# 1/sqrt in the norms: one power on GpSimd in place of nine VectorE instructions

## The chip, the cores and the metric

The kernel runs on one core of a Trainium2 chip. The metric is the device time of one execution in microseconds. The engines appear in the profile as PE (TensorE, the matmuls; PEld are its weight loads), DVE (VectorE), ACT (ScalarE), POOL (GpSimd) and SP (SyncE, which issues the DMAs). A line number such as L257 is a line of the kernel before the change.

## The reference

Two sequences of 512 tokens with 1024 channels pass through two layers that share their weights. One layer is:

```
h = RMSNorm(x);  z = h W_in, split into four groups: S5 | Hyena | RWKV-7 | neighbourhood attention
x += W_out concat_g(RMSNorm_g(mixer_g(z_g)))
x += W2 relu(W1 RMSNorm(x))^2

def rms_norm(x, g):
    y = xf * lax.rsqrt(jnp.mean(xf * xf, axis=-1, keepdims=True) + NORM_EPS)
    return y * g
```

1/sqrt of a sum over channels is wanted per token in five kinds of places: the two norms over 1024 channels of each layer, the norm of each mixer's 256 channels, the queries and keys of the attention (per head of 64 channels), the keys of RWKV (per head; here without an epsilon, with an upper limit of 1e12 on the result), and RWKV's normalisation of its output per head.

## The kernel before

Activations lie transposed: channels on the 128 partitions, tokens along the columns, 512 columns per sequence. The matrices W_in, W_out, W1 and W2 are multiplied by `mm3` in three passes of split values (high times high, high times low, low times high), each a 128x512 matmul (L1432 to L1434). `load_w` brings a block of weights; at the first use ScalarE casts the high part (L297) and GpSimd, for every fourth block VectorE, subtracts to get the low part (L298), which is also stored for the second sequence. These splits are the larger part of GpSimd's work.

Several Python generators are stepped in turn: one emits the dense stream (W_in, W_out, the MLP of both layers and sequences), one RWKV and S5, then Hyena and attention, of each sequence and layer. The program's final order on each engine isn't this one: `tile.TileContext(nc, schedule_with_timeline_sim=True)` has a planner order the instructions of every engine ahead of the run by a simulated timeline. On the chip every engine works through its own list in that order and waits at semaphores where an operand isn't ready.

A sum over channels is a sum over partitions, so it goes through TensorE. `token_rstd` multiplies squared values by a column of ones (or by a selector of the two heads) at L271, which puts tokens on the partitions: the sums of 512 tokens are 128 partitions by 4 columns, times 2 for two heads, times 2 for two chunks. L275 scales them and adds the epsilon into a tile `rsq_x`. `rsqrt` then makes `rsq_y` from it, with two helper tiles `rsq_t` and `rsq_u`, in nine small VectorE instructions (L249 to L257): a first guess by arithmetic on the bits, a step of higher order, and a Newton step. The result, tokens on partitions, has to come back to one value per column, and there are two ways: `bcast` (L293) transposes each column of `rsq_y`, repeated 128 times, on TensorE, used by the norm over 1024 channels (`norm_rstd`, whose result ScalarE copies at L1475 into the tile `R`) and by the norms of the four mixers (`group_norm`); `head_bcast` (L283) first spreads the values by a ScalarE copy and then transposes. The queries' 1/rms is used where it lies, as a scalar per partition, at L1349.

`R` scales what comes out of the next dense blocks: L1489 to L1517 for W_in, L1575 for W1. Two buffers (`pd`) take these blocks' results, so TensorE can run two blocks ahead of `R`.

Per sequence and layer there are 12 calls of `rsqrt`: two norms over 1024 channels, four mixer norms, four for queries and keys (two chunks each), and two for RWKV; with two sequences and two layers, 48.

Of the kernel before, what the change touches and what calls it, by code (L numbers as in the profile page):

```python
# [7 lines left out]
I32 = mybir.dt.int32  # L8
AF = mybir.ActivationFunctionType
ALU = mybir.AluOpType  # L10
AX = mybir.AxisListType
MUL, ADD, SUB, MAX, MIN = ALU.mult, ALU.add, ALU.subtract, ALU.max, ALU.min
P = 128
# [180 lines left out]
class Ctx:  # L194
# [46 lines left out]

    def rsqrt(self, x, n, tag):


        V = self.nc.vector
        y = self.t([P, 32], "rsq_y" + tag, 3)[:, :n]
        t = self.t([P, 32], "rsq_t" + tag)[:, :n]
        u = self.t([P, 32], "rsq_u" + tag)[:, :n]
        V.tensor_scalar(out=y.bitcast(I32), in0=x.bitcast(I32), scalar1=-0.5, scalar2=float(0x5f378000), op0=MUL, op1=ADD)  # L249
        V.tensor_tensor(out=t, in0=y, in1=x, op=MUL)  # L250
        V.tensor_tensor(out=t, in0=t, in1=y, op=MUL)
        V.tensor_scalar(out=u, in0=t, scalar1=0.3740864098072052, scalar2=-1.249273657798767, op0=MUL, op1=ADD)
        V.tensor_tensor(out=u, in0=u, in1=t, op=MUL)
        V.scalar_tensor_tensor(out=y, in0=u, scalar=1.8751890659332275, in1=y, op0=ADD, op1=MUL)
        V.scalar_tensor_tensor(out=t, in0=y, scalar=-0.5, in1=x, op0=MUL, op1=MUL)
        V.tensor_tensor(out=t, in0=t, in1=y, op=MUL)
        V.scalar_tensor_tensor(out=y, in0=t, scalar=1.5, in1=y, op0=ADD, op1=MUL)  # L257
        return y

    def token_rstd(self, srcs, ntok, sel, add, tag, sc=1.0, mulc=None):  # L260


        nc = self.nc
        nt = ntok // P
        w = sel.shape[1]
        k = 1 if w == 1 else len(srcs)
        o = self.p([P, nt, k, w], tag)
        for tt in range(nt):
            for i, s in enumerate(srcs):
                acc = w == 1  # L270
                nc.tensor.matmul(out=o[:, tt, 0 if acc else i], lhsT=s[:, tt * P:tt * P + P], rhs=sel,  # L271
                                 start=(not acc or i == 0), stop=(not acc or i == len(srcs) - 1))
        n = nt * k * w
        x = self.t([P, 32], "rsq_x" + tag, 2)[:, :n]
        nc.vector.tensor_scalar(out=x, in0=o.rearrange("p a b c -> p (a b c)"), scalar1=sc, scalar2=add,  # L275
                                op0=MUL, op1=ADD)
        return self.rsqrt(x, n, tag)

    def head_bcast(self, rn, M, tag):
# [1358 lines left out]
def trunk(tc, A, O):  # L1638
    nc = tc.nc
    base = place(nc)  # L1640
    with tc.tile_pool(name="sb", bufs=1) as sb, \
            tc.tile_pool(name="ps", bufs=1, space=bass.MemoryType.PSUM) as ps, \
            tc.tile_pool(name="dr", bufs=1, space=bass.MemoryType.DRAM) as dr:
        K = Ctx(tc, base, sb, ps, dr, A)
# [7 lines left out]
        K.zp = [K.t([P, S + 2], f"zp{b}") for b in range(2)]  # L1652
        for z in K.zp:
            nc.gpsimd.memset(z, 0.0)
        pars = [K.load_params(0)]
        zs, ys, taken, done = {}, {}, {}, set()
        xs = {(0, b): A['xT'][:, seqs[b]] for b in range(2)}
# [213 lines left out]
```

## Time and profile before

| | |
|---|---|
| median of 3 runs | 3195.2 us (3182.29 to 3195.77) |
| the profiled execution, its own time | 3179.4 us |
| its span, first to last instruction | 3177.6 us |
| mean granted TensorE clock | 0.950 of full speed |
| busy: PE, DVE, ACT, POOL | 2951.0, 1973.0, 1051.9, 828.9 us |
| HBM | 409.95 MB read, 155.83 MB written |

A busy time is the sum of an engine's instructions in the profiled execution, and its share is that of the span. In the lists of waits a row says which instruction stood, what released it, how long in total, how often, and the longest. In a timeline a row's bracket gives how long the engine had been idle ahead of it and what ended that.

### The profile page before, as it was taken

To read this page: it belongs to the slowest core of one execution; us is meant where nothing else is said; L and a number is where in the kernel's file an instruction comes from. 1 tells how busy PE (TensorE), PEld (TensorE's weight loads), DVE (VectorE), ACT (ScalarE), POOL (GpSimd) and SP (SyncE) were. 2 spreads that over 40 slices of the span, in tenths; PEclk is the share of its full clock that TensorE was granted. 3 is DMA by queue.
4 is the path that set the end of the run, shared out by engine and by line. 5 is a ranking of instruction groups with operands and counts; after the bars stand their busy time and mean duration, and the time that the engine had idled before them with its cause. 6 is when DMAs were issued, how large, how long until landed. Compare 5 with 4: busy or idle time off the path is not lost.

```text
span 3177.6 us, 48702 instructions
## 1 busy us (share of the span) xinstructions
PE 2951.0 (93%) x17328; PEld 2308.4 (73%) x17328; DVE 1973.0 (62%) x3755; ACT 1051.9 (33%) x1922; POOL 828.9 (26%) x693
## 2 busy tenths in 40 slices
PE   7987998798899998899899999998998999999999
PEld 5666776676677877767676778776776777778887
DVE  8888775785854768757627436765647457733332
ACT  5333233332322333333323223433322323332222
POOL 5642201432332336432001001312333223300000
PEclk9898999898999999999999999999999999999999
DMA  7577574365554546766655545577556445556565
GB/s 221 164 232 201 189 210 131 117 169 165 151 163 145 173 161 207 227 191 201 186 151 157 173 150 182 196 211 221 181 170 181 152 162 181 178 178 194 192 193 195
DMA packets 482840, 571.92 MB, mean 180 GB/s; under 512 B 187910, under 2 KB 238726, under 8 KB 481576
## 3 DMA queue, kind: packets, MB, share of 16 engines
q1 hardware_dynamic: 482600, 568.81, 58.4%
q8 instruction: 139, 2.28, 0.3%
q14 instruction: 101, 0.83, 0.1%
HBM read 409.95 MB, written 155.83 MB: 178 GB/s over the span
## 4 chain that ended last, share of the span: by engine, by line
PE 64%; DVE 16%; DMA 9%; issue 4%; SPq 3%; ACT 2%; POOL 1%; DVEq 0%; ACTq 0%; POOLq 0%
PE pd L1432 16%; PE pd L1434 16%; PE pd L1433 15%; DVE m L1195 2%; PE ra L677 2%; PE ra L675 2%; DMA m<-in_w_mlp 2%; PE ra L467 1%; DMA m<-in_w_in 1%; DVE m L864 1%; DVE m L530 1%; DVE m L298 1%; DMA m<-lo 1%; PE ra L1226 1%; PE ra L660 1%
## 5 line engine op out<-in xcount | busy, mean ns | idle before, releaser
L1432 PE MATMUL pd<-m,m 128*128 128x512 f32 x2984 | 1225.9, 412 | 91.7 <-ACT m L297 32.7
L1434 PE MATMUL pd<-m,m 128*128 128x512 f32 x2984 | 1210.2, 406 | 34.7 <-DMA m<-lo 23.6
L1433 PE MATMUL pd<-m,m 128*128 128x512 f32 x2984 | 1206.0, 404 | 2.3 <-DVE m L298 2.3
L1432 PEld LDWEIGHTS pd<-m,m 128*128 128x128 f32 x2984 | 580.4, 195 | 242.0 <-issue 46.0
L1434 PEld LDWEIGHTS pd<-m,m 128*128 128x128 f32 x2984 | 578.8, 194 | 176.0 <-DMA m<-lo 27.4
L1433 PEld LDWEIGHTS pd<-m,m 128*128 128x128 f32 x2984 | 580.6, 195 | 130.0 <-issue 8.0
L298 POOL TENSOR_TENSOR m<-m,m 128x512 fp32r<-128x512 f32 x282 | 395.7, 1405 | 736.5 <-ACT m L297 676.4
L1416 ACT CAST m<-m 128x512 fp32r<-128x512 f32 x376 | 232.8, 620 | 712.3 <-DMA m<-in_w_mlp 434.2
L297 ACT CAST m<-m 128x512 fp32r<-128x512 f32 (+1 forms) x400 | 256.9, 645 | 624.7 <-PE pd L1433 232.9
L1585 DVE TENSOR_TENSOR m<-pd,m 128x512 f32<-128x512 f32 x256 | 175.2, 686 | 262.6 <-PE pd L1434 262.2
L1575 DVE SCALAR_TENSOR_TENSOR do<-pd,R 128x512 f32<-128x512 f32 x128 | 87.7, 688 | 198.9 <-PE pd L1434 188.7
L1195 DVE TENSOR_TENSOR m<-m,m 128x512 f32<-128x512 f32 (+1 forms) x224 | 142.0, 677 | 4.5 <-POOL m L1195 3.6
L298 DVE TENSOR_TENSOR m<-m,m 128x512 fp32r<-128x512 f32 (+1 forms) x118 | 104.9, 889 | 62.9 <-ACT m L297 59.6
L298 DVE TENSOR_TENSOR m<-do,m 128x512 fp32r<-128x512 f32 x128 | 100.4, 786 | 62.1 <-ACT m L297 61.5
L297 ACT CAST m<-do 128x512 fp32r<-128x512 f32 x128 | 79.2, 620 | 137.0 <-DVE do L1576 136.8
L1576 DVE TENSOR_TENSOR do<-do 128x512 f32<-128x512 f32 x128 | 112.5, 880 | 3.0
L1456 POOL TENSOR_TENSOR m<-m 128x512 f32<-128x512 f32 x40 | 58.6, 1466 | 128.1 <-ACT m L1455 126.1
L1463 DVE SCALAR_TENSOR_TENSOR m<-m,par,m 128x512 fp32r<-128x512 f32 x64 | 65.1, 1026 | 34.2 <-ACT m L1462 34.1
L677 PE MATMUL ra<-m,m 128*64 128x64 f32 x512 | 77.8, 246 | 0.0
L1195 POOL TENSOR_TENSOR m<-m,m 128x512 f32<-128x512 f32 x32 | 49.2, 1540 | 98.1 <-DVE m L1195 54.9
L467 PEld LDWEIGHTS ra<-m,m 64*128 64x128 f32 x512 | 50.8, 201 | 32.5 <-issue 24.3
L675 PE MATMUL ra<-m,rw_st 64*64 64x64 f32 x448 | 73.8, 246 | 0.0
(359 smaller groups left out, 3489.9 us busy)
## 6 DMA issues: line engine op xcount, KB each, us to landing
m<-in_w_mlp SPq DMA_DIRECT2D x512, 256.0 KB, 2.9
lo<-m SPq DMA_DIRECT2D x376, 256.0 KB, 2.3
m<-lo SPq DMA_DIRECT2D x376, 256.0 KB, 2.7
m<-in_w_in SPq DMA_DIRECT2D x176, 256.0 KB, 3.5
m<-zr SPq DMA_DIRECT2D x36, 512.0 KB, 4.7
m<-in_w_out SPq DMA_DIRECT2D x64, 256.0 KB, 3.0
m<-in_xT SPq DMA_DIRECT2D x32, 256.0 KB, 4.5
zr<-do SPq DMA_DIRECT2D x32, 256.0 KB, 2.2
```

The source lines that it names most:

```text
L297: self.nc.scalar.copy(out=hi, in_=x)
L298: eng.tensor_tensor(out=lo, in0=x, in1=hi.bitcast(F32), op=SUB)
L675: nc.tensor.matmul(out=py[b0:b0 + 64, d, c], lhsT=st[b0:b0 + 64, d, c], rhs=ar[c][b0:b0 + 64, ch, 1], start=True, stop=False)
L677: nc.tensor.matmul(out=py[b0:b0 + 64, d, c], lhsT=uv[:, ch, c, q], rhs=sr[:, ch, 2 * c + q], start=st is None, stop=True)
L1195: eng.tensor_tensor(out=o, in0=a, in1=b, op=op)
L1416: nc.scalar.copy(out=hi, in_=raw)
L1432: K.nc.tensor.matmul(out=ps, lhsT=wh, rhs=hh, start=(i == 0), stop=False)
L1433: K.nc.tensor.matmul(out=ps, lhsT=wh, rhs=hl, start=False, stop=False)
L1434: K.nc.tensor.matmul(out=ps, lhsT=wl, rhs=hh, start=False, stop=(i == n - 1))
L1575: nc.vector.scalar_tensor_tensor(out=r, in0=ps, scalar=0.0, in1=R, op0=MAX, op1=MUL)
L1576: nc.vector.tensor_tensor(out=r, in0=r, in1=r, op=MUL)
L1585: nc.vector.tensor_tensor(out=x[m], in0=ps, in1=x[m], op=ADD)
```

## The change

`rsqrt` issues one GpSimd instruction, x to the power of a tile that holds -0.5, in place of the nine on VectorE. That tile is filled once at the start. Where `token_rstd` is called without an epsilon (the keys of RWKV), L275 takes the maximum with 1e-30 in place of adding 0. The helper tiles `rsq_t` and `rsq_u` are gone.

```
     def rsqrt(self, x, n, tag):
-        V = self.nc.vector
         y = self.t([P, 32], "rsq_y" + tag, 3)[:, :n]
-        t = self.t([P, 32], "rsq_t" + tag)[:, :n]
-        u = self.t([P, 32], "rsq_u" + tag)[:, :n]
-        V.tensor_scalar(out=y.bitcast(I32), in0=x.bitcast(I32), scalar1=-0.5, scalar2=float(0x5f378000), op0=MUL, op1=ADD)
-        V.tensor_tensor(out=t, in0=y, in1=x, op=MUL)
-        V.tensor_tensor(out=t, in0=t, in1=y, op=MUL)
-        V.tensor_scalar(out=u, in0=t, scalar1=0.3740864098072052, scalar2=-1.249273657798767, op0=MUL, op1=ADD)
-        V.tensor_tensor(out=u, in0=u, in1=t, op=MUL)
-        V.scalar_tensor_tensor(out=y, in0=u, scalar=1.8751890659332275, in1=y, op0=ADD, op1=MUL)
-        V.scalar_tensor_tensor(out=t, in0=y, scalar=-0.5, in1=x, op0=MUL, op1=MUL)
-        V.tensor_tensor(out=t, in0=t, in1=y, op=MUL)
-        V.scalar_tensor_tensor(out=y, in0=t, scalar=1.5, in1=y, op0=ADD, op1=MUL)
+        self.nc.gpsimd.tensor_tensor(out=y, in0=x, in1=self.mhalf[:, :n], op=ALU.pow)
         return y
 
     def token_rstd(self, srcs, ntok, sel, add, tag, sc=1.0, mulc=None):
...
-        nc.vector.tensor_scalar(out=x, in0=o.rearrange("p a b c -> p (a b c)"), scalar1=sc, scalar2=add,
-                                op0=MUL, op1=ADD)
+        nc.vector.tensor_scalar(out=x, in0=o.rearrange("p a b c -> p (a b c)"), scalar1=sc, scalar2=add or 1e-30,
+                                op0=MUL, op1=ADD if add else MAX)
         return self.rsqrt(x, n, tag)
...
             nc.gpsimd.memset(z, 0.0)
+        K.mhalf = K.t([P, 32], "mhalf")
+        nc.gpsimd.memset(K.mhalf, -0.5)
```

## Rows read from the trace of the kernel before

**Rows 1.** The page: busy us of each engine, share of the span, instructions
```profile
PE 2951.0 (93%) x17328; PEld 2308.4 (73%) x17328; DVE 1973.0 (62%) x3755; ACT 1051.9 (33%) x1922; POOL 828.9 (26%) x693
```
**Rows 2.** The page: the chain that ended last, share of the span by engine
```profile
PE 64%; DVE 16%; DMA 9%; issue 4%; SPq 3%; ACT 2%; POOL 1%; DVEq 0%; ACTq 0%; POOLq 0%
```
**Rows 3.** Stretches: length; busy us (instructions) by engine; PE clock, DMA share, GB/s
```profile
1200.00:1400.00 200.00, 175.19 (x870) 136.03 (x869) 150.39 (x260) 72.67 (x114) 103.58 (x91) 0.91 0.68 217
...
2800.00:3000.00 200.00, 196.86 (x868) 162.75 (x867) 66.16 (x103) 60.39 (x99) 2.58 (x2) 0.99 0.58 187
```
**Rows 4.** TensorE's waits: who waited <- for whom: total us, times, longest
```profile
PE pd L1432 <- DVE do L1575: 19.4, 6, 5.2
...
PE nm L293 <- DVE rsq_ynm L257: 10.5, 3, 6.2
PE pd L1434 <- POOL m L298: 10.0, 9, 3.9
...
PE ra L293 <- DVE rsq_yra L257: 2.1, 1, 2.1
...
PE nm L884 <- DVE m L864: 1.4, 1, 1.4
```
**Rows 5.** Line 257 by tile: count, duration ns min/median/max, first and last start
```profile
L257 DVE SCALAR_TENSOR_TENSOR rsq_yma<-rsq_tma,rsq_yma x24: 158/166/178, 414.1 to 2753.5; 128x8 f32<-128x8 f32 x16, 128x4 f32<-128x4 f32 x8
L257 DVE SCALAR_TENSOR_TENSOR rsq_yra<-rsq_tra,rsq_yra x15: 161/174/1271, 96.9 to 2767.9; 128x16 f32<-128x16 f32 x8, 128x4 f32<-128x4 f32 x7
L257 DVE SCALAR_TENSOR_TENSOR rsq_ynm<-rsq_tnm,rsq_ynm x9: 146/161/168, 47.7 to 2827.8; 128x4 f32<-128x4 f32 x9
```
**Rows 6.** VectorE's groups, lines 249 to 257, costliest and cheapest: busy us, mean ns
```profile
L249 DVE TENSOR_SCALAR rsq_yma<-rsq_xma 128x8 int32<-128x8 int32 (+1 forms) x24 | 7.4, 314 | 0.4
...
L250 DVE TENSOR_TENSOR rsq_tnm<-rsq_ynm,rsq_xnm 128x4 f32<-128x4 f32 x9 | 1.4, 159 | 0.2
```
**Rows 7.** Timeline at 649 us: start us, us, instruction [idle before <-releaser]
```profile
649.46 1.26 POOL L298 TENSOR_TENSOR m<-m,m 128x512 fp32r<-128x512 f32 x1 [2.94 <-ACT m L297]
649.52 1.23 DVE L253 TENSOR_TENSOR rsq_unm<-rsq_unm,rsq_tnm 128x4 f32<-128x4 f32 x1
```
**Rows 8.** Timeline at 2826 us, the last norm over 1024 channels
```profile
2825.99 0.16 DVE L275 TENSOR_SCALAR rsq_xnm<-nm 128x4 f32<-128x4 f32 x1 [4.27 <-PE nm L271]
...
2827.77 0.16 DVE L257 SCALAR_TENSOR_TENSOR rsq_ynm<-rsq_tnm,rsq_ynm 128x4 f32<-128x4 f32 x1
...
2830.26 0.60 PE L293 MATMUL nm<-c_eye,rsq_ynm 128*128 128x128 f32 x4
```
**Rows 9.** Timeline at 1223 us, the same norm in a crowded stretch
```profile
1222.89 0.15 DVE L275 TENSOR_SCALAR rsq_xnm<-nm 128x4 f32<-128x4 f32 x1
...
1223.41 2.24 POOL L298 TENSOR_TENSOR m<-m,m 128x512 fp32r<-128x512 f32 x1
...
1229.94 0.15 DVE L257 SCALAR_TENSOR_TENSOR rsq_ynm<-rsq_tnm,rsq_ynm 128x4 f32<-128x4 f32 x1
...
1230.24 1.08 PE L293 MATMUL nm<-c_eye,rsq_ynm 128*128 128x128 f32 x4 [6.16 <-DVE rsq_ynm L257]
```
**Rows 10.** GpSimd's groups by shape, one of VectorE: busy us, mean ns, idle before
```profile
L298 POOL TENSOR_TENSOR m<-m,m 128x512 fp32r<-128x512 f32 x282 | 395.7, 1405 | 736.5 <-ACT m L297 676.4 <-DMA m<-in_w_out 14.0 <-DMA m<-in_w_mlp 13.8
L667 POOL TENSOR_TENSOR rw_se<-rw_st,rw_ec 128x256 f32<-128x256 f32 x24 | 17.8, 744 | 173.2 <-DVE rw_st L668 130.9 <-DVE rw_st L664 41.9 <-DVE rw_ec L433 0.3
L1037 POOL TENSOR_TENSOR m<-m,m 128x1024 f32<-128x1024 f32 x4 | 10.5, 2622 | 28.9 <-DVE m L1036 15.3 <-DVE na_m L1352 13.6
L427 POOL MEMSET m<- 128x16 f32 x16 | 2.3, 146 | 69.8 <-PE ra L660 22.2 <-PE ra L286 18.0 <-DVE m L450 8.4
...
L298 DVE TENSOR_TENSOR m<-m,m 128x512 fp32r<-128x512 f32 x94 | 73.0, 776 | 45.0 <-ACT m L297 41.7 <-DMA m<-in_w_in 1.4 <-DMA zr<-do 1.2
```
**Rows 11.** GpSimd's waits: who waited <- for whom: total us, times, longest
```profile
POOL m L298 <- ACT m L297: 676.4, 193, 22.9
```

## The prediction

> **What bounds the kernel now.** I read the busy times first: TensorE works 93% of the span, VectorE 62%, GpSimd 26% [rows 1]. The span is 3177.6 us, so TensorE stands idle for 3177.6 - 2951.0 = 226.6 us in all; no change that leaves the matmuls alone can give back more than that. The chain of waits comes next: 64% of it is TensorE, 16% VectorE, 1% GpSimd [rows 2]. VectorE is therefore not the bound, but a part of TensorE's idle time is spent waiting for it. 16% of 3177.6 is about 510 us, against 1973 us of busy VectorE: one microsecond of VectorE in four lies on that chain. Third, the table by stretches shows where the rest can be found: between 1200 and 1400 us VectorE is busy 150 of 200 us and TensorE idles 25; between 2800 and 3000 us VectorE is busy 66 and TensorE idles 3 [rows 3]. The relief can only come from stretches of the first kind. Last, TensorE's own waits [rows 4]: the rows that name a VectorE instruction other than the ones removed are 16, the largest 19.4 us (the hidden layer's evacuation), the smallest 1.4 us, together 95 us. Those that name the removed instructions are the transposes that spread 1/rms over the columns: 10.5 us in three places (longest 6.2) and 2.1 us in one, 12.6 us in four.
>
> **What goes.** Each of the 48 norms (24 + 15 + 9 by the tiles' tags [rows 5]) loses nine VectorE instructions, 432 in all. Their busy time stands in 27 rows, from 7.4 us to 1.4 us [rows 6], whose sum is 98.8 us: 5.0% of VectorE's 1973. At their median of 0.166 us (0.161 to 0.174 [rows 5]) 432 would be 71.7 us; the 27 us more are stretches like the one where such an instruction begins 0.06 us after a GpSimd subtraction and ends 0.03 us after it, 1.23 us instead of 0.16 [rows 7]. Undisturbed, the nine take from the end of x at 2826.15 to 2827.93, 1.78 us [rows 8]. In a crowded stretch they are interleaved with other VectorE work: at 1223 us x is ready at 1223.04 and y only at 1230.09, 7.05 us [rows 9].
>
> **What comes.** One GpSimd power of 128 x 4, 8 or 16 elements per norm, 48 in all, and one fill of a constant at the start. The trace holds no power. The cheapest GpSimd instruction of comparable size is a fill of 128x16, 0.146 us; the dearest elementwise one is a product of 128x1024, 2.62 us; the smallest product with two inputs is 128x256, 0.744 us [rows 10]. I take 0.74 us, as this row is nearest in form, and keep 0.1 and 2.6 as ends. A hand-over between engines is about 0.15 us (y's end at 1230.09, the transpose at 1230.24 [rows 9]). A norm then costs about 1.0 us from x to y, when GpSimd is free at once.
>
> The Trainium skill (GPSIMD Engine Reference, section 4.1, Engine selection) says to keep elementwise work on VectorE, as GpSimd needs about twice the time with two inputs. The trace agrees for one instruction: the same subtraction takes 1405 ns there and 776 ns on VectorE [rows 10]. Read against this change, nine steps at that ratio would be 9 x 0.166 x 1.8 = 2.7 us, an estimate that falls on my upper end; by it the time would be about 3185 instead of 3182 us.
>
> **The sum, on the profiled execution (3179.4 us).**
> First, the four places where TensorE stands for y. At 1230 it had been idle since 1224.08 [rows 9]. GpSimd was then in a subtraction until 1225.65, so the power would end near 1226.4 and the transposes start near 1226.5: 2.5 of the 6.2 us stay, 3.7 go. The two others in that row have about 2.2 us each; there y lagged because the nine were strung out, and a power that is ready 1 us after x removes both, 4.3 us. In the fourth (2.1 us) the nine ran undisturbed; 1.78 becomes 1.0, 0.8 us. Together 8.8 of 12.6. With a power of 0.1 us it is 10.0, with 2.6 us 1.8 + 4.3 - 1.1 = 5.0.
> Second, the relief of VectorE elsewhere: 5.0% of the 95 us that TensorE waits for other VectorE work, 4.8 us. Below, it could be nothing, where what TensorE waits for was released by something else; above, see the second case.
> Third, edits that I cost at nothing. The power's 48 x 0.74 = 36 us go into GpSimd's idle 74%. If that cover is gone, it is the split of weights that suffers: TensorE waits for it 10.0 us in nine places today [rows 4], and one power ahead of each would add some 7 us. The power reads two tiles in SBUF like the subtraction of rows 7, so it can hold up a VectorE instruction as that one did: at most 36 us at VectorE's 62%, 22 us, against the 27 us of such stretches that vanish; I set these equal. The fill of the constant happens once, 0.1 us. The scaling ahead of it stays one VectorE instruction. In the last 350 us nothing is gained: there y was ready at 2827.93 and the transposes, ordered behind other matmuls, ran at 2830.26 [rows 8].
> Sum: 8.8 + 4.8 = 13.6 us, 3179.4 - 13.6 = 3165.8. The median of the runs shown is 15.8 us above the profiled execution, so 3195.2 - 13.6, about **3182 us**. The size of the power matters little: its ends give 3180 and 3185. What matters more is the order. It is made ahead of the run by a planner with modelled times, so 480 changed instructions shift the order of much that follows; I allow 15 us to either side for it, 3165 to 3198.
>
> **The rivals.**
> *VectorE's relief counts in full.* If the nine lie on the chain of waits as often as other VectorE work does (one in four), 98.8 x 0.26 = 26 us leave the chain instead of 4.8: 3195.2 - 8.8 - 26 = 3160 us. For it: VectorE's load in the crowded stretches [rows 3], and chains of 7 us for work of 1.5. Against: in only four places of 48 did TensorE wait for y at all [rows 4].
> *The power stands in GpSimd's queue* (the other side). GpSimd takes its work in order, and the head of its queue is mostly a weight split that waits for ScalarE's cast: 676 us in 193 waits, 3.5 us on the mean, 22.9 at most [rows 11]. A power behind such a split is late by that wait, and in turn a power that waits for its sums holds the splits behind it. It hits at the 24 norms whose y feeds a transpose directly (8 for the whole width, 16 for the groups), as TensorE too works in order. With half of the 24 places held for 3.5 us it costs 42 us; with the 12.6 saved, +29 us: 3225 us. It decides from a mean of 12.6 / 24 = 0.5 us per place beyond the present slack. For it: those waits. Against: the planner chooses GpSimd's order too, and the transposes came 2.3 us after y in the quiet case [rows 8], which is slack.
> *The power itself is slow.* No row excludes that a power needs many passes per element. Up to about 4 us it would hide in the slack just named at most places; at 6 us, 2 us over it, the 24 places give 48 us and the saving is gone: 3195 + 48 = 3243 us. It would also put 48 x 6 = 288 us on GpSimd (26% to 35%). For it: nothing in the trace; against: no elementwise GpSimd instruction lasts over 2.7 us.
>
> **How the numbers follow.** Forecast 0.50, full relief 0.20, queue 0.18, slow power 0.12. This kernel's measurement can tell about 0.5%, 16 us, from no change. The forecast's own range, 3165 to 3198, has its centre close to that border: 0.22 of its 0.50 is faster by more, 0.25 within, 0.03 slower. Full relief adds 0.18 to faster and 0.02 to within; the queue 0.06 to within and 0.12 to slower; the slow power 0.02 and 0.10. That is 0.40, 0.35, 0.25. The range has to reach into the cases on both sides: 3135 (full relief with an order that suits it, 25 us below 3160) to 3230 (just past the queue's 3225).
>
> **What would show it.** Right: VectorE's busy time falls by about 99 us to some 1875, GpSimd's rises by 5 to 125 us, TensorE's waits for y drop from 12.6 to about 4 us, and TensorE's busy time stays at 2951. The row of the power gives the disputed duration. The queue theory would show as waits of the transposes or of ScalarE's copies for the power, with the power starting long after x. The relief shows in TensorE's other waits for VectorE: 90 us by my sum, some 70 if it counts in full. The prediction is wrong if the power lasts over 3 us, or if TensorE's idle time moves by more than 30 us in places that have no norm near them, which would be the work of the changed order.

## The result, and the profile after

The changed kernel is slower: 3213.7 us median (3201.0 to 3224.5, 20 runs) against 3192.6 us (3178.7 to 3209.2, 20 runs). The ratio is 1.0061, 95% interval 1.0046 to 1.0076. The forecast was 3182 us, faster.

The arithmetic of the norms went as foretold. The page of the changed kernel, busy time by engine, beside [rows 1]:

```profile
PE 2963.3 (93%) x17328; PEld 2311.6 (72%) x17328; DVE 1903.1 (59%) x3323; ACT 1051.3 (33%) x1922; POOL 902.4 (28%) x742
```

VectorE is relieved by 69.9 us, GpSimd takes 73.5 us more. But TensorE, with the same 17328 matmuls, is busy 12.3 us longer, and its idle time rose as well: 3200.7 - 2963.3 = 237.4 us, where it was 226.6. So TensorE is the place to look.

The power itself (line 245 of the changed kernel): count, duration in ns as min/median/max, first and last start, shapes; then who waited for it.

```profile
L245 POOL TENSOR_TENSOR rsq_yma<-rsq_xma,mhalf x24: 1006/1636/3190, 405.1 to 2763.5; 128x8 f32<-128x8 f32 x16, 128x4 f32<-128x4 f32 x8
L245 POOL TENSOR_TENSOR rsq_yra<-rsq_xra,mhalf x15: 1007/2898/3895, 91.3 to 2787.0; 128x16 f32<-128x16 f32 x8, 128x4 f32<-128x4 f32 x7
L245 POOL TENSOR_TENSOR rsq_ynm<-rsq_xnm,mhalf x9: 1006/1017/1472, 36.5 to 2848.2; 128x4 f32<-128x4 f32 x9
...
  ACT m L271: 14.3, 8
```

It takes about 1.0 us for 4 columns, 1.6 for 8 and 2.9 for 16. By GpSimd's groups the 48 sum to 79.3 us, 1.65 us each, where I took 0.74; for 16 columns it is over my upper end of 2.6. And yet the waits that the forecast was about did shrink. TensorE's waits in the changed kernel (who waited <- for whom: total us, times, longest), beside [rows 4]:

```profile
PE pd L1420 <- ACT m L285: 35.1, 15, 12.5
PE ra L549 <- DVE m L536: 20.6, 6, 6.7
PE pd L1420 <- DVE m L1573: 15.3, 10, 3.4
...
PE ra L455 <- DVE m L439: 12.4, 6, 4.2
PE ra L259 <- DVE m L1521: 9.9, 2, 6.2
...
PE pd L1420 <- DVE do L1563: 8.7, 4, 3.2
...
PE ma L259 <- DVE m L1521: 5.2, 2, 3.2
...
PE ra L274 <- ACT m L271: 3.9, 1, 3.9
...
PE ra L281 <- POOL rsq_yra L245: 1.3, 1, 1.3
PE ma L281 <- POOL rsq_yma L245: 1.3, 1, 1.3
...
PE nm L281 <- POOL rsq_ynm L245: 1.2, 1, 1.2
```

More rows of the same list for the kernel before:

```profile
PE ra L467 <- DVE m L451: 7.4, 5, 3.3
...
PE ra L271 <- DVE m L1533: 4.3, 1, 4.3
...
PE ra L293 <- DVE rsq_tma L255: 1.5, 1, 1.5
...
PE ra L648 <- DVE rsq_yma L254: 0.6, 1, 0.6
...
PE ma L293 <- DVE rsq_yma L257: 0.4, 1, 0.4
...
PE ma L271 <- DVE m L1533: 0.2, 1, 0.2
```

The three rows on y are 3.8 us together, where the nine cost 12.6 in the rows of the prediction and 15.1 with the three short ones just shown. One wait for y is new, the row on L271. It goes by ScalarE's copy of y in `head_bcast`, behind a power of 16 columns:

```profile
591.25 2.90 POOL L245 TENSOR_TENSOR rsq_yra<-rsq_xra,mhalf 128x16 f32<-128x16 f32 x1 [12.67 <-DVE rsq_xra L263]
594.18 1.14 ACT L271 COPY m<-rsq_yra 128x512 f32<-128x512 f32 x2 [5.00 <-POOL rsq_yra L245]
...
594.85 1.97 PE L274 MATMUL ra<-c_eye,m 128*128 128x128 f32 x8 [3.89 <-ACT m L271]
```

With it, y holds TensorE up for 7.7 us. The other rows moved both ways. The wait for the hidden layer's evacuation (L1575 before, L1563 now) fell from 19.4 to 8.7 us; that for L439 (L451 before) rose from 7.4 to 12.4; and the matmuls that add up a norm's squares (L259, L271 before) now stand 15.1 us for VectorE's L1521 (L1533 before), where they stood 4.5. That is the start of a norm, ahead of every instruction that the edit touched. The last norm over 1024 channels, as in [rows 8]:

```profile
2847.93 0.16 DVE L263 TENSOR_SCALAR rsq_xnm<-nm 128x4 f32<-128x4 f32 x1 [4.39 <-PE nm L259]
2848.18 1.02 POOL L245 TENSOR_TENSOR rsq_ynm<-rsq_xnm,mhalf 128x4 f32<-128x4 f32 x1 [14.86 <-DVE rsq_xnm L263]
...
2852.21 0.60 PE L281 MATMUL nm<-c_eye,rsq_ynm 128*128 128x128 f32 x4
```

x to y is 1.1 us where it was 1.8, and the transposes run 3.0 us behind y. There is room here for a power almost four times as long.

### The profile page after: what moved, and what is told of

It reads as the page before. It is cut to its first block, busy times and chain, and to the rows that moved or that the text cites. A ratio compares the mean times of both kernels' runs of the same rounds, so it can differ in the third digit from the quotient of the medians.

```text
span 3200.7 us, 48342 instructions
## 1 busy us (share of the span) xinstructions
PE 2963.3 (93%) x17328; PEld 2311.6 (72%) x17328; DVE 1903.1 (59%) x3323; ACT 1051.3 (33%) x1922; POOL 902.4 (28%) x742
## 4 chain that ended last, share of the span: by engine, by line
PE 46%; DVE 7%; DMA 3%; issue 2%; SPq 1%; ACT 1%; POOL 0%; DVEq 0%; ACTq 0%; POOLq 0%
PE pd L1420 12%; PE pd L1422 12%; PE pd L1421 12%; PE ra L665 1%; DVE m L1183 1%; PE ra L663 1%; DMA m<-in_w_mlp 1%; PE ra L455 1%; DMA m<-lo 0%; PE ra L1264 0%; PE ra L1214 0%; DVE m L286 0%; PE ra L259 0%; DMA m<-rw_D 0%; PE ma L1332 0%
## 5 line engine op out<-in xcount | busy, mean ns | idle before, releaser
L1563 DVE SCALAR_TENSOR_TENSOR do<-pd,R 128x512 f32<-128x512 f32 x128 | 87.8, 688 | 211.8 <-PE pd L1422 204.2
L518 DVE TENSOR_TENSOR m<-m 128x1024 f32<-128x1024 f32 x32 | 65.8, 2056 | 13.2 <-DMA m<-m 7.0
L455 PE MATMUL ra<-m,m 64*128 64x128 f32 x512 | 56.3, 290 | 17.7 <-DVE m L439 12.4
```

Of the source, the lines that this page charges most:

```text
L455: nc.tensor.matmul(out=pm[q][:, ch - c2, c], lhsT=bk[c][h, ch].rearrange("p a b -> p (a b)"), rhs=ar[c][h, ch].rearrange("p a b -> p (a b) ...
```

## The experiments

The planner orders all engines ahead of the run. Matched in the traces by line, tile and occurrence, about a fifth of TensorE's 17328 matmuls stand in another relative order after than before (the expectation of the fourth experiment speaks of a third). So there are two theories. **P**: the power, by its time and its place on GpSimd, costs the 0.6%. **O**: the order into which the planner put everything else costs it. To separate the two, the first experiments plan one variant and run another: the planned order of the first is imposed on the second, engine by engine, with edges that order but need no semaphore. PLAN names the variant whose order is planned, REAL the one that runs. The core, shortened:

```
for n in want:                      # the planned order of the other variant
    i = insts[n]
    e = str(i.engine)
    if e in last:
        tc.add_manual_dep(i, last[e], NoSync, reason="order")
    last[e] = i.name
```

Lines of these kernels are 60 above those of the kernel before; the scaling of x, L275 before, is L335, and the power is L316. The imposed orders hold in the traces: matched as above, 6 of the 17328 matmuls of the first experiment stand in another relative order than in the kernel before. The nine in their own order under such edges were not run as a control; the nearest to one is the third experiment, whose edges repeat the order of after and whose time comes out level with it.

**The power in the order of before.** Edit: PLAN, REAL = "nine", "pow".

> The 48 powers on GpSimd, as in the changed kernel, but every engine's instructions in the order that the kernel before has (each power stands on GpSimd where the first of its nine stood in the joint order; nothing else moves). Theory O (the loss comes from the order into which the planner puts all the other work once the norms cost something else): 0.994 to 1.000 of the kernel before, since TensorE's 12.6 us of waits at the norms fall by about 9 and no other wait grows. Theory P (the power itself costs it, by its 1.0 to 3.0 us on GpSimd in front of others' work and by what it takes from VectorE): 1.004 to 1.012, the loss stays with the power.

Measured: 3191.1 us, ratio 0.9976 (0.9956 to 0.9997). O holds, P falls. Its waits for y:

```profile
PE nm L353 <- POOL rsq_ynm L316: 2.0, 1, 2.0
...
PE ra L353 <- POOL rsq_yra L316: 1.4, 1, 1.4
```

They total 3.4 us, and no row waits for ScalarE's copy. Here the crowded norm of [rows 9] can be followed, since the order around it is the same. The timeline of that stretch:

```profile
1229.55 0.15 DVE L335 TENSOR_SCALAR rsq_xnm<-nm 128x4 f32<-128x4 f32 x1
1230.07 2.24 POOL L358 TENSOR_TENSOR m<-m,m 128x512 fp32r<-128x512 f32 x1
1232.27 1.07 POOL L316 TENSOR_TENSOR rsq_ynm<-rsq_xnm,mhalf 128x4 f32<-128x4 f32 x1
...
1233.39 1.11 PE L353 MATMUL nm<-c_eye,rsq_ynm 128*128 128x128 f32 x4 [2.00 <-POOL rsq_ynm L316]
```

The power stands behind one subtraction of 2.24 us and TensorE waits 2.00 us, where it waited 6.16. The forecast had 2.5 us staying.

**The nine in the order of after.** Edit: PLAN, REAL = "pow", "nine".

> The nine VectorE instructions as in the kernel before, but every engine's instructions in the order of the changed kernel (the nine stand together on VectorE where the power stood in the joint order). Theory O: 1.006 to 1.014 of the kernel before, the loss is there without any power, and 9 us of norm waits come back on top. Theory P: 0.996 to 1.003, without the power the loss is gone.

Measured: 3239.0 us, ratio 1.0141 (1.0110 to 1.0173). The loss is there with no power in the kernel, and it is larger, at the upper edge of what theory O allowed. In this order nine or power makes 0.80%, 26 us (1.0141 against 1.0061), and not the 0.24% that it makes in the order of before: the worth of the work depends on the order around it. TensorE's waits for y are 9.9 us in this kernel and 2.9 by ScalarE's copy; where the rest comes from was not followed up.

**The order of after, without the power's time.** Edit: the power's operation to a product, the constant to 0.05, the order still planned with the power.

> The changed kernel with its order kept on every engine, and with a multiplication by 0.05 on GpSimd in place of the power: 1/sqrt isn't computed here. It takes the power's duration away (48 instructions of 1.65 us in the mean) and leaves its place and its waits. Theory O: 1.002 to 1.006 of the kernel before, most of the loss stays. Theory P: 0.990 to 0.999, the loss goes with the duration.

Measured: 3213.9 us, ratio 1.0058 (1.0038 to 1.0078). 1/sqrt is left out here. The largest of its three rows in GpSimd's groups (busy us, mean ns, idle before), first in the changed kernel, then here:

```profile
L245 POOL TENSOR_TENSOR rsq_yma<-rsq_xma,mhalf 128x8 f32<-128x8 f32 (+1 forms) x24 | 37.7, 1579 | 69.4 <-DVE rsq_xma L263 69.4
```

```profile
L316 POOL TENSOR_TENSOR rsq_yma<-rsq_xma,mhalf 128x8 f32<-128x8 f32 (+1 forms) x24 | 8.0, 336 | 74.7 <-DVE rsq_xma L335 74.7
```

The instruction shrank from 1579 ns in the mean to 336 and the time did not move (1.0061 for the changed kernel). In this order the power's length is worth nothing that this comparison, good to some 0.25% or 8 us, can tell. It is seen at one place, the wait by ScalarE's copy, 3.9 us with the power:

```profile
PE ra L346 <- ACT m L343: 1.2, 1, 1.2
```

**The same work in another order.** Edit, in the kernel before:

```
-        t = self.t([P, 32], "rsq_t" + tag)[:, :n]
-        u = self.t([P, 32], "rsq_u" + tag)[:, :n]
+        t = self.t([P, 32], "rsq_t" + tag, 2)[:, :n]
+        u = self.t([P, 32], "rsq_u" + tag, 2)[:, :n]
```

> The kernel before with its nine instructions, where the two scratch tiles of the nine have two buffers instead of one: the same instructions on the same engines, but the planner puts them in another order (about a tenth of TensorE's instructions move, where the change moves a third). Theory O: the time differs from before by 0.2% or more, in either direction. Theory P: within 0.2% of before.

Measured: 3224.3 us, ratio 1.0089 (1.0058 to 1.0119). No instruction was changed, added or removed; beside the order, only the waits for the reuse of the two tiles and the tiles' places in memory can differ. The loss is no smaller than that of the case. Most of TensorE's added idle time, 24 us, sits elsewhere: between the fourth and the fifth copy of R (the broadcast 1/rms of a norm) TensorE idles 39 us where it idled 19, both summed from the traces. TensorE's waits of this kernel from 1200 to 1560 us:

```profile
PE pd L1432 <- ACT m L297: 11.9, 4, 6.7
PE nm L293 <- DVE rsq_ynm L257: 9.4, 2, 5.9
PE pd L1434 <- POOL m L298: 7.7, 2, 7.0
PE ma L958 <- DMA m<-s_sB: 5.7, 2, 4.4
```

**Where in the order.** At about 600 and 1040 us of the kernel before, both orders have issued the same set of instructions, so there one can pass from one to the other. Edit: the planned order is joined from pieces ("pow" up to the cut and "nine" behind it, and so on); all with the power.

> With the powers. The order of the changed kernel for the first third of the work (up to about 1040 us of the kernel before, a point up to which both orders have issued the same set of instructions), the order of the kernel before behind it. Theory O with its loss in the first third, as the profiled segments of the changed kernel have it (some 22 us longer up to the fourth R copy than a_before_order_power, some 10 us shorter behind it): 1.003 to 1.009 of the kernel before. Theory S (the loss is spread, or is one of the clock that any order may meet): about half of it, 0.999 to 1.003.

> With the powers. The other way round: the order of the kernel before up to about 1040 us, that of the changed kernel behind it. Theory O with its loss in the first third: 0.993 to 0.998 of the kernel before, the best of both. Theory S: 1.000 to 1.004.

> With the powers. The order of the changed kernel only for the work that the kernel before does from 600 to 1040 us, where its granted clock is 0.82 to 0.92 against 0.88 to 0.96; the order of the kernel before everywhere else. Theory O with its loss there: 1.001 to 1.007 of the kernel before. Theory S: 0.996 to 1.001.

Measured: 1.0048 (1.0030 to 1.0065), 0.9991 (0.9975 to 1.0006), 1.0014 (0.9999 to 1.0030). Against a_before_order_power (0.9976) the first third of the new order costs 0.72%, the remainder 0.15%; the sum, 0.87%, is what the whole order costs (1.0061 - 0.9976 = 0.85%). The middle piece alone is 0.38%, 12 us. Each of these differences is uncertain by about 0.26%, so the remainder can't be told from nothing. Theory O with its loss in the first third holds; but I had expected the last two thirds to gain, and they don't: f lies between the ranges of the two theories.

What the order does there is seen when g and a are laid side by side; they have the same instructions and the same order up to 600 us. First the matmuls of the MLP (tile pd) in 80 us: busy us (count), granted clock, DMA share, GB/s. In the kernel before and the changed kernel:

```profile
760.00:840.00 80.00, 24.58 (x94) 0.81 0.50 146
```

```profile
760.00:840.00 80.00, 15.99 (x57) 0.68 0.40 113
```

In a_before_order_power:

```profile
760.00:840.00 80.00, 20.50 (x77) 0.77 0.45 131
```

In g_after_order_600_1040:

```profile
760.00:840.00 80.00, 14.03 (x51) 0.66 0.38 109
```

The MLP's matmuls, 128x512, are what fills TensorE between the small ones of the other stream. The new order has 51 of them in this stretch, the old one 77, and TensorE's granted clock, between its two levels of 2.4 and 1.2 GHz, is 0.66 of full on the mean and not 0.77. All other matmuls of the stretch are about as many in both (408 in a, 400 in g), so it is the filling that is missing. The four kernels that have the order of before in this stretch (before, a, f, h) have 77 to 94 of the filling matmuls and a clock of 0.77 to 0.83, the five with the order of after (after, b, c, e, g) 51 to 67 and 0.66 to 0.72. The groups from 755 to 835 us show what the clock costs, again a first and then g:

```profile
L1492 PE MATMUL pd<-m,m 128*128 128x512 f32 x28 | 12.4, 444 | 5.5 <-DVE do L1635 5.5
...
L735 PE MATMUL ra<-m,rw_st 64*64 64x64 f32 x48 | 9.4, 285 | 0.0
L737 PE MATMUL ra<-m,m 128*64 128x64 f32 x48 | 9.3, 286 | 0.0
```

```profile
L735 PE MATMUL ra<-m,rw_st 64*64 64x64 f32 x48 | 11.1, 331 | 0.0
L737 PE MATMUL ra<-m,m 128*64 128x64 f32 x48 | 11.1, 333 | 0.0
L1492 PE MATMUL pd<-m,m 128*128 128x512 f32 x19 | 8.4, 444 | 3.5 <-DVE do L1635 3.0 <-DVE m L1645 0.5
```

The same 48 matmuls take 331 ns and not 285, while those of the MLP stay at 444. In these 80 us TensorE idles some 4 us more in g (61.6 us busy against 65.8), but over the run no more than in a (table below): the loss is time at the lower clock level. The profiled execution of g is the slowest of its twelve, but the mean granted clock over all runs says the same: 0.9471 in a (12 runs), 0.9435 in g (12), 0.9401 in e (9), 0.9430 in the changed kernel (20), beside 0.946 to 0.947 for the kernel before in each series of runs. What the clock lacks to 1, times the time, is 12 us more in g than in a and 24 us more in e, as much as their mean times are longer (10 and 23 us, all give or take some 3 us); in the changed kernel it is 14 of 22 us. The Trainium skill (Perfetto Trace Analysis, section Matmul Optimizations) says that the matmul engine scales its power with its utilization, and that matmuls should therefore run back to back in batches. The two kernels fit that, as far as the granted clock shows it: where fewer filling matmuls stand between the small ones, it is lower, 0.66 against 0.77. This stretch alone doesn't make the time, though: i_loads_earlier_nine, below, has 68 and 0.71 here and is level with the kernel before.

**What the norms are worth at all.** Edit, in the order of before: `V.tensor_scalar(out=y, in0=x, scalar1=0.05, scalar2=1e-30, op0=MUL, op1=ADD)` in place of the nine.

> In the order of the kernel before, one VectorE instruction of the same form (x by 0.05, plus a constant) in place of the nine: 1/sqrt isn't computed here. This is what the norms' arithmetic costs at all: VectorE loses some 87 us of work and GpSimd gets none. If the power on GpSimd costs nothing that counts, this equals a_before_order_power, 0.995 to 0.999 of the kernel before. If the power's microseconds on GpSimd cost it, this is lower by them: 0.988 to 0.994.

Measured: 3187.4 us, ratio 0.9972 (0.9958 to 0.9986). 1/sqrt is left out here too. The power, 80 us of GpSimd, is level with one VectorE instruction (0.9976), within some 0.25%, which fits that GpSimd's idle time hides it. And all that the nine cost in this order is about 0.28%, 9 us.

**Was that order bad luck?** Two constants of the planner's priorities were changed, each for the nine and for the power as they stand: `OFF_W` from 0 to 300, then `OFF_M` from 0 to 300.

> The kernel before with one constant of the planner's priorities changed: the weight loads of the MLP and their splits count as 300 places earlier (OFF_W 0 to 300). Same instructions, other order (a fifth of TensorE's instructions move). Theory O: any of 0.995 to 1.015 of the kernel before, and what matters is its pair, i_loads_earlier_power.

> The changed kernel with the same constant (OFF_W 300): the same edit, drawn in another order. Theory O: the edit's effect, this over i_loads_earlier_nine, can be anything from 0.985 to 1.012 and need not be the 1.006 of the case. Theory P (the edit itself costs): 1.004 to 1.009 again.

> The kernel before with another constant changed: the MLP's steps count as 300 places later (OFF_M 0 to 300). Same instructions, a tenth of TensorE's move. Theory O: any of 0.995 to 1.015 of the kernel before, and what matters is its pair, l_mlp_later_power.

> The changed kernel with the same constant (OFF_M 300). Theory O: this over k_mlp_later_nine anything from 0.985 to 1.012. Theory P: 1.004 to 1.009 again.

Measured: 1.0002, 1.0038; 1.0016, 1.0072. Power over nine is 1.0036 and 1.0056, near the 1.0061 of the case. Theory P had 1.004 to 1.009, theory O allowed almost anything and so gains nothing by it. The pairs speak for P, or for a bias of the planner, and against a draw without one. The next four tell these apart: the power in the two orders that were planned with the nine, and in two more orders planned with other stand-ins.

> The power, in an order that the planner made with a multiplication on GpSimd in its place. Draw theory D (each edit draws an order from a spread, and the kernel before has one of the best): anything from 0.995 to 1.010. Rule theory R (orders planned with VectorE freed of the nine are worse as a rule, by some 0.8%): 1.004 to 1.009. Theory C (it is the power's cost in the plan that spoils it): 0.996 to 1.001.

> The power, in an order that the planner made with one VectorE instruction in place of the nine. Theory D: anything from 0.995 to 1.010. Theory R: 1.004 to 1.009. Theory C: 0.996 to 1.001.

> OFF_W 300, the order planned with the nine (that of i_loads_earlier_nine, 1.0002), run with the power. If the power by itself gains what it gained in the order of the kernel before (0.24%): 0.996 to 0.999, and 0.5 to 0.8% below j_loads_earlier_power, which the planner's order alone then makes. If it gains only in that one order: 1.000 to 1.003.

> OFF_M 300, the order planned with the nine (that of k_mlp_later_nine, 1.0016), run with the power. If the power gains 0.24% again: 0.998 to 1.001, and 0.6 to 0.9% below l_mlp_later_power. If it gains only in the order of the kernel before: 1.001 to 1.004.

All orders in one table, as ratios to the kernel before, each against runs of it made alongside; the half widths are 0.14 to 0.32%:

```
order planned with ...            run with the nine   run with the power
the nine (the case)                    1                 0.9976
the nine, OFF_W 300                    1.0002            0.9993
the nine, OFF_M 300                    1.0016            1.0023
the nine, two scratch buffers          1.0089            -
the power (the case)                   1.0141            1.0061
the power, OFF_W 300                   -                 1.0038
the power, OFF_M 300                   -                 1.0072
a GpSimd product                       -                 1.0058
one VectorE instruction                -                 1.0065
```

Read along the first three rows: nine or power is within 0.24% either way. With OFF_W the power in the nine's order is 0.45% below the one that was planned for it, with OFF_M 0.49%, a little less than the 0.5 to 0.8% and 0.6 to 0.9% that I expected, so the loss in these pairs is nearly all the order's and not the power's; but the gain of 0.24% over the nine did not come again (p lies where I had put "only in the order of the kernel before", o between the two cases). Read down the last column: five orders planned without the nine, all slower, by 0.4 to 0.7%, and the stand-in matters little. So it is not the power's price in the plan (theory C falls). A draw without bias (D) isn't excluded by any one of them, but would rarely put five of five on one side; the five are related plans, though, three of them with the same constants. That plans without the nine are worse as a rule (R) fits them, but the two scratch buffers show that a plan with the nine can be worse still. Nor was it tested whether the planner's constants simply suit the nine. Why the planner does worse here, I did not find.

## Why the prediction was wrong

**The waits for y: nearly right.** Forecast from 12.6 to about 3.8; the changed kernel has 3.8 at the transposes that the prediction counted, the power in the old order 3.4, and the place at 1223 us came within half a microsecond. The count was short on both sides: three rows, 2.5 us, of the kernel before were left out, and so was the way by ScalarE's copy, 3.9 us in the changed kernel. From 15.1 to 7.7 us is the whole of it.

**The relief of VectorE: not the large case, and the small one isn't seen.** The two terms were 13.6 us together. The order of before gives 0.24% with the power, 8 us (1 to 14), and 0.28% with one instruction, 9 us (4 to 13). The rival with full relief (35 us) is out. But the 4.8 us of relief are not shown either: TensorE's other waits for VectorE, all rows summed, are 98.0 us in the kernel before, 106.1 in a and 110.0 in the changed kernel, where the forecast let them fall. The waits for y alone fell by 11.7 us in a, which is as much as was gained. In the two other orders planned with the nine the power gained 0.1% and lost 0.1%, each uncertain by about 0.26%; while in the order of after it gained 0.80%; so I would not claim the 8 us for any other order. VectorE fell to 1903, not to 1875: its remaining work took some 29 us more, for instance the weight splits of line 298 (286 after) 930 ns each instead of 889. That is not the power's length, since VectorE is at 1908 with the short product too (c).

**The power's price: wrong, and all but harmless.** 1.65 us instead of 0.74. The sum said that its size matters little; c, a and h bear that out within their 8 us. The sentence on the Trainium skill (GPSIMD Engine Reference, section 4.1, Engine selection) went by its ratio of about two for an elementwise operation, 1.8 in the trace, for each of nine steps and had 2.7 us. The rows agree with that estimate only for 16 columns: the power goes by columns, 1.0 to 2.9 us.

**The queue: not here.** A power behind a subtraction was seen (2.24 us, above), but the waits for y are 3 to 8 us in all, not 42.

**The order: this is the step that failed.** The forecast said that "480 changed instructions shift the order of much that follows; I allow 15 us to either side for it". It measured 0.85% between a and the changed kernel, 27 us, to one side. I had treated it as noise around zero without a reason, and all five plans without the nine came out on the bad side. The range (3135 to 3230) held the time of 3213.7 us by luck: the queue's rival, which didn't happen, had widened it. The sign to watch for that I wrote down, TensorE's idle time moving by over 30 us far from norms, also missed half of it: idle rose by 10.8 us only, because the order acts through the clock as well. The clock stood nowhere in the prediction. It took TensorE's idle time, 226.6 us, for the most that could be won back and its busy time for fixed at 2951 us; the same matmuls took 2963.3. With the profiled span, TensorE's busy time and the mean clock of each kernel (time lost to the clock, an estimate, is the span times what the clock lacks to 1):

```
                        span    TensorE idle   lost to the clock   rest
before                 3177.6      226.6           158.9          2792
a_before_order_power   3187.6      225.0           165.8          2797
after                  3200.7      237.4           172.8          2790
g_after_order_600_1040 3208.5      224.6           192.5          2791
b_after_order_nine     3228.0      257.2           180.8          2790
d_same_work_other      3227.5      251.0           187.2          2789
```

The rest is the same within 8 us; what an order costs is in the two columns of the middle, and either can carry it. These are single executions, and the clock differs between executions of one kernel too (0.938 to 0.953 in those of the kernel before), which is why the verdicts above go by medians, and the clock's share by the means over all runs.

**The version that beats both** is the power in the order planned with the nine: 0.24% faster than before (0.03 to 0.44%), 0.85% faster than the change as it stands.

## What to carry to other kernels

Where a planner orders the program, an edit has two effects, and they can be measured apart by imposing the old order on the new instructions. Here the work was worth -0.24% in the old order, and the order then +0.85%. The two do not simply add: taken the other way round, the order costs 1.41% with the nine, and the work is then worth -0.80%. Before costing microseconds at the changed lines, take the spread that the same work has in other orders (here 0 to 1.4% for the nine) as the error of the forecast, and don't centre it at zero when the order before is the best one known: every other order tried with the same work was level or slower.

## What the hardware showed that I had not expected

A power on GpSimd costs mostly by the column: medians of 1.02, 1.64 and 2.90 us for 4, 8 and 16 columns, against 0.20 to 0.22 us in the median for a product of the same tiles in c. And TensorE's clock turned an order of instructions into time without a wait: in g the clock from 600 to 1040 us is lower than in a,

```profile
600.00:1040.00 440.00, 395.38 (x2599) 305.96 (x2599) 264.89 (x441) 128.77 (x242) 144.48 (x105) 0.87 0.51 147
```

```profile
600.00:1040.00 440.00, 398.03 (x2653) 309.87 (x2653) 274.84 (x451) 131.06 (x247) 151.80 (x109) 0.91 0.52 152
```

(g first; busy us and counts by engine, then the clock): 54 fewer matmuls in the same 440 us, with TensorE busy for only 2.7 us less.
